# Hybrid attention block on one core: the state space's phasor step is squared once on GpSimd, and the first layer's parameters are issued later

## The chip, the cores and the metric

The kernel runs on one core of a Trainium2 chip. The metric is the device time of one execution in microseconds, from the program's start to its end. Three runs of the kernel before gave 1392.8, 1395.85 and 1401.91 us; the median is 1395.85 us.

## What is computed

Two layers of a hybrid block over 528 positions (16 meta tokens and 512 of the sequence) and 1024 channels. Each layer normalises, projects to three mixers (stick-breaking attention, retention, a state-space mixer), projects back, and adds a gated MLP. The part that the change touches is the state-space mixer:

```python
dt = jnp.exp(log_dt.astype(f32))[:, None]
mag = jnp.exp(lr * dt)
ar = mag * jnp.cos(li * dt)
ai = mag * jnp.sin(li * dt)
...
bu_r = jnp.einsum('lbgc,gpc->lbgp', ug, bbr)
bu_i = jnp.einsum('lbgc,gpc->lbgp', ug, bbi)
_, _, xr, xi = lax.associative_scan(_complex_affine_combine, (a_r, a_i, bu_r, bu_i), axis=0)
y = (jnp.einsum('lbgp,gcp->lbgc', xr, c_re.astype(f32))
     - jnp.einsum('lbgp,gcp->lbgc', xi, c_im.astype(f32)))
```

## The kernel before, in words

All activations are held transposed, channels on partitions and the 528 positions along the free dimension, in 60 shared slots. Matrix products of the weights are made in three passes (`mm3`: weight and input are each split into a rounded and a remaining part), in two halves of 264 columns; their accumulators are called `pj`. Weights come one unit at a time by DMA on SP's queue into two buffers (`wr`), are rounded on ScalarE (`wh`) and their rest taken on VectorE or GpSimd (`wl`).

A layer runs 23 units of projection in the order of `PROJ`, then the output projection in three parts (`OUT_PARTS`; in layer 0: stick-breaking, state space, retention), then the MLP. Everything else is written as generators (`spawn`), and `tick`, called after each weight product, resumes those that are due. Whether one is due goes by a clock that the building program keeps for each engine: `spend` adds the estimated duration of each instruction, and a task may go on once its own time is not later than TensorE's clock plus 200. So the estimates set the order in which instructions are written; after that the tile framework orders them once more, by a simulated time line with that order as priority, and each engine executes its list in order.

`first_params` (line 1046) runs from the start of the kernel: `s5_scalars` makes cosine, sine and magnitude of the states for both layers at once on VectorE (16 columns, 8 for each layer; `cu`, `su`, `mg`, in tiles `s5w` and `s5p`), then `s5_params` for layer 0 loads the matrices (`braw`) and starts five tasks: `inputs` twice (`btmp`, `ws`, `wps`, `we`), `outputs` (`gx`, `gg`, `bbd`, `kps`, `tz`) and `phasors` twice, one for each half of the states. For layer 0 the first half goes to VectorE and the second to GpSimd; layer 1's parameters are computed during layer 0's MLP, both halves on GpSimd.

`phasors` builds the powers of the chunk step's phasor, 132 of them for each state, by doubling: it holds the step's current power in `st` (4 columns), multiplies the powers so far (`phr`, `phi`, by way of `py`) by it, and squares it (lines 684 to 689). The list `par` is filled when all five tasks are over, and the state-space lane `s5_lane` of the layer (`uc`, `es`, `xr`, `xi`, `yps`, `ysm`, then `glu`) waits for it. The attention of a pair of heads waits for `sq`, `sk`, `sv` of that pair (the first two normed by `headnorm`); its scores are made in `z`, those of the retention in `sc` and its result in `ro`.

Of the kernel before, what the change touches and what calls it, by code (L numbers as in the profile page):

```python
# [8 lines left out]
F32 = mybir.dt.float32  # L9
# [3 lines left out]
ALU = mybir.AluOpType  # L13
PSUM = bass.MemoryType.PSUM

P = 128
# [21 lines left out]
NCH = T // Q  # L38
# [12 lines left out]
def width(g):  # L51
    return g[-1][3] + g[-1][2] - g[-1][1]
# [36 lines left out]
def hybrid_kernel(ctx, tc, A, out, dbg=None):  # L89
# [6 lines left out]
    def spend(key, ns):  # L96
        t = now[0]
        start = max(busy[key], busy["PE"])
        if t:
            if key != t[3]:  # L100
                t[3], t[4] = key, t[1]
            start = max(start, t[4])
            t[1] = max(t[1], start + ns + HOP)
        busy[key] = start + ns
# [21 lines left out]
    G = Timed(nc.gpsimd, "G", 110, 2.1)  # L126

    def mm(out, lhsT, rhs, start, stop, more=False):

        n = out.shape[-1] / 2.4  # L130
        spend("PE", 2 * max(107.0, 2 * n) if rhs.dtype == F32 else max(107.0, n) + 3)
        nc.tensor.matmul(out, lhsT=lhsT, rhs=rhs, start=start, stop=stop, skip_group_check=more)  # L132

    class TE:
# [5 lines left out]
    cp = ctx.enter_context(tc.tile_pool(name="cp", bufs=1))  # L140
# [12 lines left out]
    def nm(s):  # L153
        uid[0] += 1
        return f"{s}_{uid[0]}"

    def tt(s="t"):
        return tp.tile([P, T], F32, tag="t", name=nm(s))
# [58 lines left out]
    def const(shape, dt, name):  # L217
        return cp.tile(shape, dt, tag=name, name=name)
# [9 lines left out]
    for name, g in (("A", G_A), ("B2", G_B2)):  # L228
        n = width(g)
        m = masks[n] = const([P, n], BF16, "mask" + name)  # L230
        G.memset(m, 0.0)
        for j, q0, q1, o0 in g:
            c = slice(o0, o0 + min(q1 - q0, P))
# [111 lines left out]
    def mm3(ps, w, x, c0=0, nt=T, first=True, last=True, ticks=TICKS):  # L345

        a, b = w
        xh, xl = x
        kt = len(xh)
        for k in range(kt):  # L350
            for i, (wt, xt) in enumerate(((a, xh), (a, xl), (b, xh))):
                for p, (c, n) in zip(ps, spans(nt)):
                    mm(p[:, :n], lhsT=wt[:, k, :], rhs=xt[k][:, c0 + c:c0 + c + n],
                       start=first and k == 0 and i == 0, stop=last and k == kt - 1 and i == 2)
                tick(ticks)
# [24 lines left out]
    class Norm:  # L380
# [28 lines left out]
        def finish(self):  # L409
            a, b = self.acc  # L410
            for i in range(2):
                ps = bank("nps")
                c = slice(HALF * i, HALF * i + HALF)
                mm(ps[:, :HALF], lhsT=meanw, rhs=a[:, c], start=True, stop=False)
                mm(ps[:, :HALF], lhsT=meanw, rhs=b[:, c], start=False, stop=True)
                rs_from(ps[:, :HALF], self.rr, HALF * i, HALF)
            rs_exp(self.rr)
# [32 lines left out]
    def s5_scalars():  # L450
# [79 lines left out]
        mul(fi, t1, den)  # L530
        return cu, su, mg, ar, ai, fr, fi

    def s5_params(l, engines, scal, par):

        def on(eng):
            return (lambda o, a, b, op=op: eng.tensor_tensor(out=o, in0=a, in1=b, op=op)
                    for op in (ALU.mult, ALU.add, ALU.subtract))

        cu, su, mg, ar, ai, fr, fi = scal
        m_ = lambda t, a: t[:, 16 * a + 8 * l:16 * a + 8 * l + 8]  # L540
        fr, fi = m_(fr, 0), m_(fi, 0)
        braw = tt("braw")
# [26 lines left out]
        mul, add, sub = on(engines[0])  # L569
# [88 lines left out]
        def phasors(hf):  # L658

            eng = engines[hf]  # L660
            mul, add, sub = on(eng)
            p3 = lambda t: t.rearrange("p (t n) -> p t n", n=NCH)
            pr, pi, y1, y2 = tt("phr"), tt("phi"), tt("py"), tt("py")
            for t, v in ((pr, 1.0), (pi, 0.0)):
                G.memset(p3(t)[:, :, 0:1], v)
            st = cp.tile([P, 16], F32, tag=f"st{hf}", name=nm("st"))
            sr, si = st[:, 0:4], st[:, 4:8]
            ua, ub = st[:, 8:12], st[:, 12:16]
            eng.tensor_copy(out=sr, in_=m_(cu, 4)[:, 4 * hf:4 * hf + 4])
            eng.tensor_copy(out=si, in_=m_(su, 4)[:, 4 * hf:4 * hf + 4])  # L670
            n = 1
            while n < NCH:
                yield
                c = min(n, NCH - n)
                bs = lambda a: a.rearrange("p (t o) -> p t o", o=1).to_broadcast([P, 4, c])
                a1, a2 = p3(y1)[:, :, :c], p3(y2)[:, :, :c]
                mul(a1, p3(pr)[:, :, 0:c], bs(sr))
                mul(a2, p3(pi)[:, :, 0:c], bs(si))
                sub(p3(pr)[:, :, n:n + c], a1, a2)
                mul(a1, p3(pr)[:, :, 0:c], bs(si))  # L680
                mul(a2, p3(pi)[:, :, 0:c], bs(sr))
                add(p3(pi)[:, :, n:n + c], a1, a2)
                n *= 2
                if n < NCH:
                    mul(ua, sr, sr)
                    mul(ub, si, si)
                    mul(si, sr, si)
                    sub(sr, ua, ub)
                    add(si, si, si)
            ph[hf] = (pr, pi)  # L690
            over.append("phasors")

# [3 lines left out]
        for g in (inputs(0), inputs(1), outputs(), phasors(0), phasors(1)):  # L696
            spawn(g, now[0][1])
# [348 lines left out]
    def first_params():  # L1046
        yield
        scal.extend(s5_scalars())
        yield
        yield from s5_params(0, (V, G), scal, par)  # L1050

    scal = []
    spawn(first_params())
    for l in range(LAYERS):
        got = {}
# [95 lines left out]
        for n, (kind, i, f0, nf) in enumerate(mlp_order()):  # L1151
# [17 lines left out]
            if n == 3 and not last:  # L1169
                par = []  # L1170
                spawn(s5_params(l + 1, (G, G), scal, par), busy["G"])
# [101 lines left out]
```

## Time and profile before

| | |
|---|---|
| median of three runs | 1395.85 us (1392.8 to 1401.91) |
| the profiled execution's own time | 1399.35 us |
| its span, first to last instruction | 1397.6 us |
| mean granted TensorE clock | 0.990 |
| TensorE busy | 1370.0 us |
| VectorE busy | 807.1 us |
| ScalarE busy | 618.9 us |
| GpSimd busy | 509.2 us |

In the profile's rows PE is TensorE's matrix product and PEld its weight load, DVE is VectorE, ACT ScalarE, POOL GpSimd, SP the queue that issues the DMAs. Nearly all instructions of VectorE, ScalarE and GpSimd are recorded by one helper (line 121) and all matrix products by another (line 132), so they are told apart by the names of their tiles: `out<-in`.

### The profile page before, as it was taken

Reading aid. Unit: us, or ns where it says so; the run is one execution under the profiler, and the core shown is the slowest. Engines: PE = TensorE matmul, PEld = TensorE weight load, DVE = VectorE, ACT = ScalarE, POOL = GpSimd, SP = SyncE. Lnnn points to the kernel's source line nnn. Section 1 sums busy time; section 2 is a strip of 40 time slices with the busy share of each in tenths; the row PEclk is TensorE's granted clock in tenths of the full one; section 3 lists DMA queues with packets and bytes.
Section 4 is the critical chain, followed back from the end, with each engine's and each line's share of the span. In section 5 each row is a group of like instructions: output and inputs, shape, how many; then the busy total and the mean of one; then the engine's idle time right before and its main releaser. Section 6 shows DMA issues by size and latency. Waiting matters only on the chain.

```text
span 1397.6 us, 22767 instructions
## 1 busy us (share of the span) xinstructions
PE 1370.0 (98%) x9188; PEld 1254.3 (90%) x9188; DVE 807.1 (58%) x1312; ACT 618.9 (44%) x1002; POOL 509.2 (36%) x624
## 2 busy tenths in 40 slices
PE   6999999999999999999999999999999999999998
PEld 6989898999999999999999999998788888888886
DVE  8875557767455545544566477464585543553453
ACT  5456565545343223322354564874363432442231
POOL 5685536322689302200233544362122210220020
PEclk9999799999999999999999999999999999999999
DMA  4212102313221322222222121122232322223223
GB/s 154 69 65 96 38 21 84 97 46 115 97 76 61 106 91 91 90 93 87 80 91 91 61 93 46 56 68 82 79 106 96 100 92 94 101 91 104 93 77 105
DMA packets 38985, 118.27 MB, mean 85 GB/s; under 512 B 4960, under 2 KB 5472, under 8 KB 38880
## 3 DMA queue, kind: packets, MB, share of 16 engines
q1 hardware_dynamic: 38880, 116.82, 25.8%
q8 instruction: 72, 1.18, 0.3%
q14 instruction: 33, 0.27, 0.1%
HBM read 111.46 MB, written 2.10 MB: 81 GB/s over the span
## 4 chain that ended last, share of the span: by engine, by line
PE 85%; DVE 8%; POOL 4%; issue 1%; DMA 1%; ACT 1%; SPq 0%; DVEq 0%; POOLq 0%; ACTq 0%
PE pj L132 71%; PE z L132 6%; PE hps L132 1%; PE ro L132 1%; PE av L132 1%; DVE s5w L121 1%; PE sc L132 1%; PE yps L132 1%; DVE wl L121 1%; POOL lo L121 1%; PE kps L132 1%; DVE sq L121 1%; DVE gg L121 1%; DVE fr L121 0%; PE kv L132 0%
## 5 line engine op out<-in xcount | busy, mean ns | idle before, releaser
L132 PE MATMUL pj<-xh,wh 128*128 128x264 f32 (+1 forms) x1792 | 451.5, 311 | 13.7 <-ACT wh L121 5.2
L132 PE MATMUL pj<-xh,wl 128*128 128x264 f32 (+1 forms) x1792 | 451.6, 311 | 1.6 <-DVE wl L121 1.6
L132 PE MATMUL pj<-xl,wh 128*128 128x264 f32 (+1 forms) x1792 | 449.7, 310 | 1.7 <-DVE xl L121 1.7
L121 ACT CAST wh<-wr 128x1024 fp32r<-128x1024 f32 (+3 forms) x209 | 206.0, 987 | 417.5 <-PE pj L132 381.8
L132 PEld LDWEIGHTS pj<-xh,wh 128*128 128x128 f32 x1792 | 298.3, 191 | 31.3 <-issue 7.5
L132 PEld LDWEIGHTS pj<-xl,wh 128*128 128x128 f32 x1792 | 298.5, 190 | 19.6 <-DVE xl L121 2.4
L132 PEld LDWEIGHTS pj<-xh,wl 128*128 128x128 f32 x1792 | 298.2, 190 | 19.3 <-issue 2.0
L121 DVE TENSOR_TENSOR wl<-wr,wh 128x1024 fp32r<-128x1024 f32 (+3 forms) x166 | 249.2, 1502 | 73.7 <-ACT wh L121 71.3
L132 PE MATMUL pj<-hi,wh 128*128 128x264 f32 (+1 forms) x720 | 192.9, 323 | 0.0
L132 PE MATMUL pj<-lo,wh 128*128 128x264 f32 (+1 forms) x720 | 192.3, 321 | 0.0
L132 PE MATMUL pj<-hi,wl 128*128 128x264 f32 (+1 forms) x720 | 191.7, 321 | 0.1
L121 POOL TENSOR_TENSOR up<-ga,up 128x528 f32<-128x528 f32 (+1 forms) x44 | 61.8, 1405 | 345.6 <-DVE up L121 345.6
L121 DVE TENSOR_TENSOR h<-h,pj 128x264 f32<-128x264 f32 (+1 forms) x144 | 69.2, 511 | 135.1 <-PE pj L132 135.0
L121 POOL TENSOR_TENSOR wl<-wr,wh 128x1024 fp32r<-128x1024 f32 (+2 forms) x43 | 95.6, 2223 | 130.4 <-ACT wh L121 122.9
L132 PEld LDWEIGHTS pj<-hi,wh 128*128 128x128 f32 x720 | 119.4, 188 | 11.0 <-ACT wh L121 0.6
L132 PEld LDWEIGHTS pj<-hi,wl 128*128 128x128 f32 x720 | 119.4, 188 | 10.9 <-DVE wl L121 0.5
L132 PEld LDWEIGHTS pj<-lo,wh 128*128 128x128 f32 x720 | 119.4, 188 | 10.3
L121 POOL TENSOR_TENSOR lo<-ga,hi 128x528 fp32r<-128x528 f32 (+1 forms) x44 | 58.9, 1339 | 158.7 <-ACT hi L121 158.6
L121 DVE TENSOR_TENSOR up<-pj,R 128x264 f32<-128x264 f32 (+1 forms) x66 | 32.2, 515 | 95.2 <-PE pj L132 95.2
L121 ACT ACTIVATE si<-si,bias 128x528 f32<-128x528 f32 (+1 forms) x44 | 32.1, 731 | 94.3 <-DVE si L121 94.3
L121 DVE TENSOR_TENSOR ga<-si,up 128x528 f32<-128x528 f32 (+1 forms) x44 | 31.7, 720 | 72.7 <-ACT si L121 56.8
L121 ACT ACTIVATE e<-z 128x512 f32<-128x512 f32 (+2 forms) x72 | 39.3, 546 | 63.2 <-PE z L132 57.2
(228 smaller groups left out, 1747.1 us busy)
## 6 DMA issues: line engine op xcount, KB each, us to landing
wr<-in_w_in_dram SPq DMA_DIRECT2D x45, 512.0 KB, 3.5
wr<-in_w_gate_dram SPq DMA_DIRECT2D x44, 512.0 KB, 3.4
wr<-in_w_up_dram SPq DMA_DIRECT2D x44, 512.0 KB, 3.4
wr<-in_w_down_dram SPq DMA_DIRECT2D x32, 512.0 KB, 3.4
wr<-in_w_out_dram SPq DMA_DIRECT2D x16, 384.0 KB, 3.2
wr<-in_w_down_dram SPq DMA_DIRECT2D x16, 384.0 KB, 3.1
rc<-in_rope_dram SPq DMA_DIRECT2D x12, 264.0 KB, 3.7
rs<-in_rope_dram SPq DMA_DIRECT2D x12, 264.0 KB, 4.0
```

The source lines that it names most:

```text
L121: return f(*a, **k)
L132: nc.tensor.matmul(out, lhsT=lhsT, rhs=rhs, start=start, stop=stop, skip_group_check=more)
```

## The change

Three edits. The squarings of the step's phasor leave `phasors`; a new function `s5_steps` makes the eight powers at once for all 16 columns (both layers, both halves) on GpSimd, right after the scalars, and `phasors` reads them from its tile `s5s`. `first_params` then goes on to `s5_params` only when `sq` and `sk` of pair 0 are in `got`, that is, normed. And the building program's estimate for a matrix product with 64 rows or 64 output partitions is halved.

```diff
     def mm(out, lhsT, rhs, start, stop, more=False):
 
         n = out.shape[-1] / 2.4
-        spend("PE", 2 * max(107.0, 2 * n) if rhs.dtype == F32 else max(107.0, n) + 3)
+        t = 2 * max(107.0, 2 * n) if rhs.dtype == F32 else max(107.0, n) + 3
+        spend("PE", t / 2 if 64 in (rhs.shape[0], out.shape[0]) else t)
...
+    def s5_steps(scal):
+
+        W = 16
+        steps = cp.tile([P, 8 * 2 * W], F32, tag="s5s", name="s5s")
+        tmp = cp.tile([P, 2 * W], F32, tag="s5t", name="s5t")
+        ua, ub = tmp[:, :W], tmp[:, W:]
+        at = lambda i, c: steps[:, W * (2 * i + c):W * (2 * i + c) + W]
+        for c in range(2):
+            G.tensor_copy(out=at(0, c), in_=scal[c][:, 4 * W:5 * W])
+        for i in range(1, 8):
+            r, m = at(i - 1, 0), at(i - 1, 1)
+            G.tensor_tensor(out=ua, in0=r, in1=r, op=ALU.mult)
+            G.tensor_tensor(out=ub, in0=m, in1=m, op=ALU.mult)
+            G.tensor_tensor(out=at(i, 0), in0=ua, in1=ub, op=ALU.subtract)
+            G.tensor_tensor(out=ua, in0=r, in1=m, op=ALU.mult)
+            G.tensor_tensor(out=at(i, 1), in0=ua, in1=ua, op=ALU.add)
+        return steps
...
-            st = cp.tile([P, 16], F32, tag=f"st{hf}", name=nm("st"))
-            sr, si = st[:, 0:4], st[:, 4:8]
-            ua, ub = st[:, 8:12], st[:, 12:16]
-            eng.tensor_copy(out=sr, in_=m_(cu, 4)[:, 4 * hf:4 * hf + 4])
-            eng.tensor_copy(out=si, in_=m_(su, 4)[:, 4 * hf:4 * hf + 4])
             n = 1
-            while n < NCH:
+            for i in range(8):
                 yield
                 c = min(n, NCH - n)
+                o = 32 * i + 8 * l + 4 * hf
+                sr, si = steps[:, o:o + 4], steps[:, o + 16:o + 20]
...
                 n *= 2
-                if n < NCH:
-                    mul(ua, sr, sr)
-                    mul(ub, si, si)
-                    mul(si, sr, si)
-                    sub(sr, ua, ub)
-                    add(si, si, si)
...
         scal.extend(s5_scalars())
         yield
+        scal.append(s5_steps(scal))
+        yield lambda: ("sq", 0) in got and ("sk", 0) in got
         yield from s5_params(0, (V, G), scal, par)
```

## Rows read from the trace of the kernel before

**Rows 1.** The page: busy us by engine; the chain that ended last.

```profile
...
PE 1370.0 (98%) x9188; PEld 1254.3 (90%) x9188; DVE 807.1 (58%) x1312; ACT 618.9 (44%) x1002; POOL 509.2 (36%) x624
...
PE 85%; DVE 8%; POOL 4%; issue 1%; DMA 1%; ACT 1%; SPq 0%; DVEq 0%; POOLq 0%; ACTq 0%
...
```

**Rows 2.** Busy us by stretch: length, each engine (instructions), clock, DMA share, GB/s.

```profile
...
34.00:110.00 76.00, 71.37 (x538) 66.70 (x537) 58.59 (x155) 37.04 (x67) 58.80 (x125) 1.00 0.20 67
...
154.00:158.00 4.00, 2.86 (x20) 2.23 (x18) 4.00 (x5) 1.31 (x4) 4.00 (x3) 1.00 0.32 116
158.00:176.00 18.00, 18.00 (x77) 16.11 (x76) 4.07 (x13) 9.54 (x20) 7.44 (x7) 0.53 0.09 29
...
381.00:391.00 10.00, 6.42 (x33) 6.24 (x33) 6.90 (x10) 3.07 (x4) 9.77 (x16) 0.66 0.16 55
...
740.00:980.00 240.00, 239.37 (x1802) 224.51 (x1801) 145.05 (x261) 144.94 (x277) 107.62 (x76) 1.00 0.22 70
...
```

**Rows 3.** What TensorE waited for: us in total, times, longest us.

```profile
...
PE pj L132 <- DVE ga L121: 3.6, 1, 3.6
...
PE pj L132 <- DVE py L121: 2.0, 1, 2.0
...
PE vps L138 <- DVE rg L121: 1.1, 1, 1.1
...
PE kps L132 <- POOL bbd L121: 0.8, 1, 0.8
...
PE z L132 <- DVE u L121: 0.8, 1, 0.8
...
```

**Rows 4.** Tile st, 30:110 and 400:475 us: ns min/median/max, first, last start.

```profile
...
L121 POOL TENSOR_TENSOR st<-st x39: 188/200/249, 32.1 to 106.6; 128x4 f32<-128x4 f32 x39
L121 DVE TENSOR_TENSOR st<-st x35: 147/157/2351, 32.4 to 86.5; 128x4 f32<-128x4 f32 x35
...
L121 POOL TENSOR_TENSOR st<-st x66: 188/197/1326, 408.0 to 463.7; 128x4 f32<-128x4 f32 x66
...
```

**Rows 5.** VectorE in order of time: start, us, what, idle before.

```profile
...
33.90 2.33 DVE L121 TENSOR_TENSOR s5w<-s5p,cols 128x16 f32<-128x16 f32 x1
...
43.47 3.48 DVE L121 TENSOR_TENSOR gx<-braw,s5p 128x640 f32<-128x640 f32 x2 [3.62 <-DMA braw<-in_bc_dram]
...
53.30 0.76 DVE L121 SCALAR_TENSOR_TENSOR sq<-sq,cols,hsq 128x528 f32<-128x528 f32 x1
...
60.95 1.15 DVE L121 SCALAR_TENSOR_TENSOR sk<-sk,cols,hsq 128x528 f32<-128x528 f32 x1
...
```

**Rows 6.** GpSimd in order of time, 28 to 100 us.

```profile
...
33.80 2.40 POOL L121 TENSOR_TENSOR wl<-wr,wh 128x1024 fp32r<-128x1024 f32 x1 [1.09 <-ACT wh L121]
...
43.14 2.40 POOL L121 TENSOR_TENSOR wl<-wr,wh 128x1024 fp32r<-128x1024 f32 x1 [6.79 <-ACT wh L121]
...
72.01 0.21 POOL L121 TENSOR_TENSOR py<-phi,st 128x16 f32<-128x16 f32 x1
...
```

**Rows 7.** SP's DMA issues in order of time, 0 to 420 us.

```profile
...
38.22 0.42 SPq L543 DMA_DIRECT2D braw<-in_bc_dram  x1
45.57 79.22 SPq L283 DMA_DIRECT2D wr<-in_w_in_dram  x9
...
```

**Rows 8.** ScalarE in order of time, 38 to 62 us.

```profile
...
50.72 0.67 ACT L121 ACTIVATE hsq<-hsq 128x528 f32<-128x528 f32 x1
...
```

**Rows 9.** TensorE, then VectorE, in order of time near 150 us.

```profile
...
140.93 2.03 PE L132 MATMUL z<-sq,sk 64*128 64x256 f32 x10
...
150.63 2.39 DVE L121 TENSOR_TENSOR xi<-fr,phi 128x528 f32<-128x528 f32 x1
152.94 1.62 DVE L121 TENSOR_TENSOR y<-fi,phr 128x528 f32<-128x528 f32 x1
...
```

**Rows 10.** Tile glu until 310 us; VectorE in order of time after 300.

```profile
...
L121 DVE TENSOR_TENSOR lo<-glu,hi x2: 698/698/699, 287.4 to 288.1; 128x528 fp32r<-128x528 f32 x2
...
304.19 0.77 DVE L121 TENSOR_TENSOR h<-h,pj 128x264 f32<-128x264 f32 x2 [4.27 <-PE pj L132]
...
```

## What the change was expected to do

> **What bounds the kernel now.** I read the page first, then the busy time by stretch, then TensorE's waits, and only then single instructions of the stretches that stood out. TensorE is busy for 98% of the span and carries 85% of the chain that ended last [rows 1]. The change adds no matmul and takes none away, so it can only give back, or add, time in which TensorE idles or runs at its lower clock. That time is small and lies in few places [rows 2]. From 34 to 110 us, where the first layer's parameters are computed, 76.00 - 71.37 = 4.6 us are idle. From 154 to 158 us 1.14 us are idle, and right behind it TensorE runs 18 us at a mean granted clock of 0.53, which is the 1.2 GHz level for most of it: 18 x 0.47 = 8.5 us lost. Around 381 us, in the first layer's MLP, 3.6 us are idle and the clock is 0.66 for the 10 us: 3.4 us more. The second layer's projections and attention, the same code in another order, lose 0.6 us in 240. So some 18 us could come back after the start-up, and 1% is 14 us.
>
> The waits name the causes [rows 3]: 2.0 us on `py` and 0.8 us on `u` (VectorE, in the stretch of the phasors), 1.1 us on `rg` (the idle time ahead of the slow clock), 3.6 us on `ga` (the MLP), 0.8 us on `bbd` (GpSimd, second layer's parameters).
>
> **Part 1, the squarings.** In the kernel before each of four phasor tasks squares its step 7 times (NCH is 132), in 5 instructions each: 35 on VectorE and 35 on GpSimd for layer 0, 70 on GpSimd for layer 1. The counts agree: 35 on VectorE, 39 + 66 = 105 on GpSimd [rows 4]. At the medians the removal is 35 x 0.157 = 5.5 us of VectorE and 105 x 0.20 = 21 us of GpSimd, of which 14 us fall into the MLP. Eight copies go too (6 on GpSimd, 2 on VectorE, under 0.3 us each). Added are 35 products and 2 copies of 128x16 on GpSimd, before anything else of the parameters. The nearest row is a 128x16 product on GpSimd, 0.21 us [rows 6]: 37 x 0.21 = 7.8 us in one dependent chain. It can start where the old squarings did, at 32.1 us [rows 4], and GpSimd has nothing but one `wl` of 2.40 us until 43.1 (6.79 us idle before that one) [rows 6]. 32.1 + 7.8 + 2.4 = 42.3: it fits in the gap, cost nothing. Without that cover the cost is at most 7.8 us of start for the parameters, which have the slack worked out in part 2.
>
> VectorE pays for GpSimd's work, though. A 128x16 product of the scalars took 2.33 us beside GpSimd's 2.40 us `wl` [rows 5, 6]. If each of the 37 new GpSimd products held VectorE for its own length, the last scalars and the reads of the first projections out of PSUM, which follow them on VectorE, would come up to 7.8 us later; the scalars are nearly done by then, so I keep half of it, +4, for the range and take 0, because TensorE's waits on VectorE in that stretch are for `py` and `u` alone, far behind [rows 3]. The Trainium skill ("GPSIMD Engine Reference", Key points) says that GpSimd shares its SBUF interfaces with VectorE and contends with VectorE instructions that have two SBUF inputs; the 2.33 us agree with that. By that rule alone moving small products to GpSimd is no relief for VectorE, and the forecast would be 4 us higher.
>
> What do the 5.5 us bring in layer 0? They are taken from between the PSUM reads that TensorE waited for: bound 0 (another VectorE instruction ends last) to 2.0 + 0.8 = 2.8 us. In layer 1 the 14 us of GpSimd are in the MLP, where TensorE waits once, 0.8 us for `bbd`: bound 0 to 0.8; I take all of it, because `bbd`'s copies stand among the squarings on the same queue.
>
> **Part 2, the wait.** Now `braw` is asked for at 38.2 and the first product `gx` starts at 43.5 [rows 5, 7]. With the wait the load and everything behind it (products for the input and output matrices, transposes, `kps`, phasors) is issued after `sq` and `sk` of pair 0 are normed. The norm of `sk` is at 60.95, but the exponential that it needs was done at 50.72 + 0.67 = 51.4 [rows 5, 8]: 9.5 us were lost behind parameter products, and `sq` had the like at 53.3. Freed of these, `sk` is done near 52. The load stands in SP's queue behind weight loads that each wait for a free buffer; the next nine took 79 us to issue, 8.8 us each [rows 7], so it moves by one or two places: 45.6 to 54 us. The parameters then start 8 to 16 us later (I take 10), and the last phasor step, near 106.6 now [rows 4], ends at 106 + 10 - 7 (35 x 0.20 that GpSimd no longer does) = 109, at worst 116. Queued behind the load on SP are weights, with three units of lead.
>
> Who waits for the parameters? The state-space lane of layer 0, which ends with `lo` of `glu` at 288.8; TensorE takes up those rows only for the second part of the output projection. The last sum of the first part into `h` is at 304.2 [rows 10]. Slack 15 us: +3 (or +10) costs nothing.
>
> What does TensorE gain early? VectorE keeps all the parameter work but 5.5 us; it only runs it later, between the PSUM reads of pairs 1 and 2. Both ends: 0 to 2.8 us as above. I take 1.0, since most of the work that delays the reads is only moved.
>
> What is late next is the jam at 150 us. The wait for `rg` comes from two state-space products on VectorE, `xi` 2.39 us and `y` 1.62 us beside GpSimd work [rows 9], that stand ahead of the read of `rg`. Their lane now comes some 3 to 10 us later against the projections, and the order around it changes too (part 3). I take the idle 1.1 us and the slow stretch of 8.5 us as gone: -9.6; the other end is 0.
>
> **Part 3, the price of a 64-row matmul.** No instruction changes, but the program that writes the kernel advances its TensorE clock by half as much for the products of `z`, `sc` and `ro`. Per layer that is 6 x 2.64 (three `G_A`, two `G_B1`, three `G_B2` matmuls a head) + 3 x 2.14 + 3 x 2.14 = 28.7 us before, 14.3 now. Ten such matmuls of `z` took 2.03 us [rows 9]; the old price of the ten is 3.47 us, the new one 1.74. So the new price is nearer, and every due time in both attentions moves: the order of instructions there is redrawn, that of the MLP is not. What an order is worth is bounded by the two layers: 9.6 us lost to one jam in layer 0, 0.6 in layer 1 [rows 2]. So 0 to -9.6 for layer 0 (the same jam as in part 2, not a second gain) and 0 to +9.6 for layer 1. I take 0 here.
>
> **Sum.** Against the profiled execution's own 1399.35 us (span 1397.6 and 1.75 around it; 3.5 above the median 1395.85): -1.0 -0.8 -9.6 = 1388.0 us.
>
> **Rivals.**
> A, the forecast: the slow stretch at 158 us goes, the MLP's stop stays. 1388, own range 1383 to 1393.
> B, the slow stretch stays, or an equal one appears elsewhere in layer 0: the work only moves. For it: VectorE and GpSimd keep nearly all their work in this layer. Against it: the products that made it are moved. 1399.35 - 1.8 = 1397.5. That the change does nothing at all (the load would come late anyway) gives the same.
> C, the MLP's stop at 381 us goes as well: 1388 - 3.6 - 3.4 = 1381. For it: GpSimd is full there. Against: the squarings come after 404 us (first at 408.0 [rows 4]), the stop before them.
> D, slower: the state-space lane is the late one. It decides from the point where it ends more than 15 us later than now; with parameters 25 us late TensorE idles 10 us before the second part of the output projection and, as at 381 us, runs slowly behind it, 3.4: 1397.5 + 13.4 = 1411. Against it: I find 3 to 10 us.
> E, slower: the new order gives layer 1 a jam like that of layer 0 while layer 0 keeps its own: 1397.5 + 9.6 = 1407.
>
> **Chances.** A 0.40, B 0.27, C 0.14, D 0.07, E 0.12. The median before may hold fewer slow stretches than the profiled execution (it is 3.5 us below), which spreads A and B by as much. 1380 to 1406 leaves out the lower part of C (0.07), most of D (0.06) and the upper part of E (0.06). A measurement of this kernel can tell about 1%, 14 us, from no change: faster means below 1381.9 (half of C and the lower edge of A, 0.13), slower above 1409.8 (half of D and the edge of E, 0.07), same 0.80.
>
> **What would show it.** Right: 37 products of 128x16 on GpSimd before the first `gx`, no `st` rows of the phasors; `gx` first at 51 to 60 us; the norms of `sq` and `sk` before 53; last phasor step at 106 to 116; no stretch at 0.5 clock between 150 and 180; the idle time near 381 us unchanged; the same PE instructions, 9188. Wrong: parameters later than 120 us, a clock below 0.9 in any stretch of layer 1, idle TensorE near 300 us, or new idle time between 60 and 110 us above 5 us.

## The result, and the profile after

The changed kernel takes 1407.24 us (median of 12, 1403.0 to 1410.79) against 1395.7 us before in the same session (median of 12): ratio 1.0085, 95% interval 1.0067 to 1.0104. It is slower by 11.5 us; the forecast was 1388.0 us, and 1407.24 lies just outside the range of 1380 to 1406. The profiled execution's own time is 1410.79 us, its span 1409.1 us, mean granted clock 0.984.

Of the 12 executions the profiled one took longest; its span, too, is 11.5 us longer than the one before (1397.6). Where these went is read from the first `nps` matmul of each stage, the sums of a norm (us, one profiled execution each):

| | start | layer 0, mixers | layer 0, MLP | layer 1, mixers | layer 1, MLP |
|---|---|---|---|---|---|
| before | 34.6 | 311.3 | 394.2 | 298.5 | 359.0 |
| after | 36.2 | 316.0 | 398.4 | 297.7 | 360.8 |

The kernel after, busy us by stretch (columns as in [rows 2]):

```profile
...
34.00:110.00 76.00, 71.09 (x464) 66.93 (x464) 53.56 (x108) 37.11 (x68) 53.27 (x102) 0.87 0.18 60
...
88.00:108.00 20.00, 19.23 (x78) 18.04 (x79) 5.81 (x18) 7.59 (x14) 7.67 (x17) 0.50 0.08 26
...
158.00:176.00 18.00, 18.00 (x151) 17.88 (x150) 14.35 (x25) 9.48 (x17) 12.71 (x12) 1.00 0.25 83
300.00:314.00 14.00, 12.15 (x62) 9.69 (x61) 4.74 (x11) 6.84 (x14) 1.31 (x1) 0.63 0.00 0
386.00:396.00 10.00, 6.40 (x40) 6.21 (x39) 6.91 (x10) 2.61 (x4) 9.85 (x15) 0.83 0.19 54
428.00:440.00 12.00, 8.40 (x45) 7.01 (x44) 3.38 (x5) 3.60 (x5) 11.76 (x27) 0.72 0.29 89
750.00:990.00 240.00, 239.37 (x1799) 224.33 (x1799) 141.90 (x262) 145.15 (x276) 105.05 (x75) 1.00 0.22 69
...
```

The 1.6 us of the first column cannot be put down to the change: over the 20 kernels of the next table that column lies between 34.0 and 37.7 us. The slow stretch of 158 to 176 us [rows 2] is gone: clock 1.00. One of the same size stands at 88 to 108 us, at 0.50 (the 1.2 GHz level), 19.23 x 0.50 = 9.6 us lost. New are the slow stretch at 300 to 314 us and the stop at 430 us. Layer 1's mixers are as clean as before. TensorE's waits after (to be held against [rows 3]):

```profile
...
PE pj L133 <- DVE ga L121: 3.6, 1, 3.6
PE kps L133 <- POOL bbd L121: 3.6, 1, 3.6
...
PE pj L133 <- DVE sq L121: 3.1, 1, 3.1
...
PE pj L133 <- DVE rg L121: 1.2, 1, 1.2
PE hps L133 <- ACT hsq L121: 1.1, 1, 1.1
...
```

`py` is gone, `sq` has come (VectorE reads a projection out of PSUM at 88.29 us, TensorE goes on at 88.77), and `bbd` went from 0.8 to 3.6 us. The three stops that matter here, TensorE in order of time, after:

```profile
...
88.77 0.59 PE L133 MATMUL pj<-xh,wh 128*128 128x264 f32 x1 [3.13 <-DVE sq L121]
...
301.37 1.32 PE L133 MATMUL ro<-sc,rv 128*64 128x128 f32 x10 [0.73 <-DVE sc L121]
...
307.76 2.12 PE L133 MATMUL hps<-hsq,blk 128*128 128x264 f32 x4 [1.09 <-ACT hsq L121]
...
```

VectorE and GpSimd around the wait for `sq`, in order of time, after:

```profile
...
78.46 0.23 DVE L121 TENSOR_TENSOR py<-phr,s5s 128x64 f32<-128x64 f32 x1
78.60 2.43 DVE L121 TENSOR_TENSOR py<-phi,s5s 128x64 f32<-128x64 f32 x1
80.95 0.76 DVE L121 TENSOR_TENSOR u<-pj,R 128x264 f32<-128x264 f32 x2
...
83.46 1.32 DVE L121 TENSOR_TENSOR py<-phi,s5s 128x64 f32<-128x64 f32 x1
...
88.29 0.42 DVE L121 TENSOR_TENSOR sq<-pj,R 128x264 f32<-128x264 f32 x1
...
```

```profile
...
78.53 2.42 POOL L121 TENSOR_TENSOR wl<-wr,wh 128x1024 fp32r<-128x1024 f32 x1 [0.24 <-ACT wh L121]
...
81.30 5.49 POOL L121 TENSOR_TENSOR lo<-sp,hi 128x432 fp32r<-128x432 f32 x5
...
```

Pair 0's attention, now ahead of the parameters, puts five `lo` on GpSimd at 81.3 us; beside them phasor products of 128x64 on VectorE take 0.9 to 1.3 us, where the one at 78.46 us takes 0.23, and the read of `sq` stands behind them.

### The profile page after: what moved, and what is told of

Same layout as the page of the kernel before. It is cut to its first block, busy times and chain, and to the rows that moved or that the text cites. A ratio compares the mean times of both kernels' runs of the same rounds, so it can differ in the third digit from the quotient of the medians.

```text
span 1409.1 us, 22670 instructions
## 1 busy us (share of the span) xinstructions
PE 1375.4 (98%) x9188; PEld 1258.3 (89%) x9188; DVE 800.1 (57%) x1275; ACT 620.3 (44%) x1002; POOL 491.1 (35%) x550
## 3 DMA queue, kind: packets, MB, share of 16 engines
q8 instruction: 72, 1.18, 0.3%
## 4 chain that ended last, share of the span: by engine, by line
PE 88%; DVE 6%; POOL 3%; issue 1%; ACT 1%; DMA 0%; SPq 0%; DVEq 0%; POOLq 0%; ACTq 0%
PE pj L133 73%; PE z L133 7%; PE hps L133 2%; PE ro L133 2%; PE av L133 1%; POOL py L121 1%; DVE s5w L121 1%; PE yps L133 1%; PE sc L133 1%; DVE py L121 1%; PE kps L133 1%; DVE wl L121 0%; PE es L133 0%; POOL lo L121 0%; POOL gx L121 0%
## 5 line engine op out<-in xcount | busy, mean ns | idle before, releaser
L133 PE MATMUL pj<-xl,wh 128*128 128x264 f32 (+1 forms) x1792 | 454.6, 311 | 2.7 <-DVE xl L121 2.7
L121 ACT CAST wh<-wr 128x1024 fp32r<-128x1024 f32 (+3 forms) x209 | 206.1, 988 | 433.8 <-PE pj L133 392.2
L121 DVE TENSOR_TENSOR wl<-wr,wh 128x1024 fp32r<-128x1024 f32 (+3 forms) x166 | 244.2, 1472 | 74.1 <-ACT wh L121 70.2
L121 POOL TENSOR_TENSOR up<-ga,up 128x528 f32<-128x528 f32 (+1 forms) x44 | 62.0, 1409 | 359.8 <-DVE up L121 355.6
L121 ACT ACTIVATE e<-z 128x416 f32<-128x416 f32 (+2 forms) x72 | 39.1, 546 | 52.1 <-PE z L133 51.2
```

The costliest lines, as they stand in the source:

```text
L121: return f(*a, **k)
```

## The experiments

All kernels in one table. "wps" is the first `we` (ScalarE's copy of the parameters' transposes), "ssm" and "ret" the last `lo` of `glu` and of `o` (ends of the state-space and the retention lane), "MLP at" the first `nps` of the first MLP, "MLP" its length, "bbd" TensorE's wait for it; all us, one profiled execution each. The ratio is to the kernel before on the same chip, with its interval; in it 0.001 is 1.4 us. The places come from one execution: that of the changed kernel, of e6_layer0_only, of e11 and of e6_price_wait was the longest of its kernel (by 3.6, 5.2, 5.0 and 3.2 us over the median), so there they may lie some us late.

| kernel | ratio | wps | ssm | ret | MLP at | MLP | bbd |
|---|---|---|---|---|---|---|---|
| before | 1 | 70.6 | 288.1 | 311.2 | 345.9 | 394.2 | 0.8 |
| after | 1.0085 (1.0067-1.0104) | 100.3 | 307.0 | 318.1 | 352.2 | 398.4 | 3.6 |
| e1_price | 0.9994 (0.9978-1.0009) | 70.0 | 289.4 | 313.1 | 340.0 | 393.1 | 1.3 |
| e2_squarings | 1.0068 (1.0048-1.0087) | 107.8 | 302.9 | 312.7 | 346.8 | 397.9 | 3.6 |
| e3_wait | 1.0002 (0.9985-1.002) | 100.2 | 300.2 | 311.7 | 343.4 | 392.8 | 1.4 |
| e4_sq_wait | 1.0077 (1.0057-1.0097) | 98.1 | 294.9 | 321.6 | 348.2 | 398.3 | 3.5 |
| e5_chain_unused | 1.0033 (1.0018-1.0047) | 108.5 | 297.2 | 320.8 | 347.4 | 393.3 | 1.2 |
| e6_layer0_only | 1.0041 (1.0025-1.0056) | 107.1 | 311.6 | 321.5 | 355.6 | 393.7 | 1.2 |
| e7_layer1_only | 1.0061 (1.0044-1.0077) | 109.9 | 297.4 | 321.0 | 347.6 | 396.9 | 3.6 |
| e8_bbd_early | 1.003 (1.0017-1.0042) | 100.2 | 304.1 | 315.4 | 349.5 | 392.0 | - |
| e9_chain_unpriced | 0.9994 (0.9978-1.001) | 71.3 | 284.6 | 307.8 | 342.4 | 394.7 | 1.1 |
| e10_clock_only | 1.0051 (1.0031-1.0071) | 111.4 | 304.6 | 312.1 | 347.5 | 393.3 | 1.4 |
| e11_sq_unpriced | 1.0061 (1.0038-1.0083) | 72.9 | 304.6 | 319.9 | 349.7 | 397.5 | 3.6 |
| e12_price_sq_unpriced_early | 1.0001 (0.9984-1.0019) | 72.2 | 282.1 | 305.9 | 340.8 | 392.8 | - |
| e6_price_wait | 1.0155 (1.013-1.0179) | 100.9 | 316.5 | 340.5 | 367.8 | 392.9 | 1.2 |
| e13_price_sq_early | 0.9993 (0.9981-1.0006) | 97.3 | 294.3 | 310.8 | 340.7 | 392.2 | - |
| e14_price_gv | 0.9995 (0.998-1.001) | 70.7 | 292.4 | 316.1 | 343.1 | 392.6 | - |
| e15_price_sq_gv | 1.0054 (1.0035-1.0072) | 70.0 | 286.8 | 310.7 | 345.3 | 396.7 | - |
| e16_e13_ggup | 0.9971 (0.9956-0.9985) | 99.3 | 296.4 | 312.9 | 342.8 | 389.5 | - |
| e17_e12_ggup | 1.0001 (0.9985-1.0017) | 70.5 | 283.5 | 307.3 | 342.0 | 390.7 | - |

The times that missed what was expected: e2, e7 and e10 came 0.4 to 1.5 us above theirs (1406.5, 1405.4, 1404.3 us), e6_layer0_only (1404.3) and e16 (1392.0) between the two ranges given, e15 (1403.1) 7 us above both, e6_price_wait (1417.3) 14 us above; e11 and e17 are taken up below.

### One part alone: e1_price, e2_squarings, e3_wait, e4_sq_wait

Each is the kernel before with the hunks of the change named: the two lines of `mm`; `s5_steps` and the new loop of `phasors`; the line with `got`; the last two together.

> Only the halved estimate for 64-row products; squarings in place, no wait. Theory P (the estimate redraws the order, and the new order makes the new stops): TensorE idles near 81 to 89 us and runs at 0.5 clock behind it, and the time is near that of the changed kernel, 1404 to 1409 us. Theory W (the wait brings pair 0's attention forward into the phasors and so makes the stop at 85 us): no idle time above 2 us between 80 and 110 us, first z near 80 us as before, time 1393 to 1398. Theory S (the squarings at once shift GpSimd's work in the MLP): no stop at 430 us here, kps waits at most 1 us; time 1393 to 1398.

> Only the squarings, made once on GpSimd; no wait, old estimate. Theory S: the stop of 3.6 us on bbd near 430 us and the half clock behind it are there, 3.6 + 3.3 = 7 us, and the parameters of layer 0 start as late as in the changed kernel (bb products near 55 to 60 us); time 1400 to 1405. Theory P and theory W: no stop on bbd above 1 us; the jam at 150 to 176 us is as before; time 1393 to 1398.

> Only the wait for the norms of pair 0; squarings in place, old estimate. Theory W: the norms of sq and sk come by 52 us, the first z near 58 us instead of 80, the stop of some 3 us and 20 us at 0.5 clock between 81 and 110 us are there, those at 150 to 176 us are gone, time within 3 us of the kernel before (1393 to 1399). Theory P and theory S: first z near 80 us, jam at 150 us as before, time 1393 to 1398; the places tell them apart, not the time.

> Squarings and wait, old estimate: the change without its third edit. Theory P: the early stop at 81 to 110 us and the one at 430 us are gone or halved, time 1393 to 1399. Theory W with S: both stops are there, time 1403 to 1409, the estimate is worth nothing.

The estimate alone and the wait alone change nothing that can be measured; the squarings alone cost 0.68%, with the wait 0.77%, which is not told apart from 0.68. Theory P falls: an early stop (5.9 us, on `u`) is in e4 too, without the halved estimate. The wait does what theory W said, and where: in e3 the norms have started by 52 us, the first `z` is at 58.5, TensorE waits 6.4 us for `u` at 81 to 88 us, and the jam at 150 us is gone, with a net of nothing. The jam is no mark of the wait alone, though: e1 and e2 do not have it either (clock 1.00 from 158 to 176 us). Theory S holds as to `bbd`: 3.6 us in e2 and e4, 1.3 and 1.4 in e1 and e3. Its other half does not: in e2 GpSimd's chain does not keep VectorE's first `gx` back (42.7 us, before 43.5), and the `bb` products start at 48.9 us, not at 55 to 60.

### Which layer, and the chain itself: e5_chain_unused, e6_layer0_only, e7_layer1_only

```diff
-            n = 1
-            for i in range(8):
...
+            if False:
+                n = 1
+                for i in range(8):
...
+            else:
...
+                n = 1
+                while n < NCH:
...
```

The cut is from e5, against the changed kernel; e6_layer0_only has `if l == 0:` there and e7 `if l == 1:`. The first loop reads the steps from `s5s`, the second squares in `st` as before; all three go without the wait and with the old estimate.

> The kernel before, with the chain of 37 products and copies of 128x16 on GpSimd written out after the scalars, but not used: every phasor task squares for itself as before; no wait, old estimate. Theory C (the chain itself, in GpSimd's queue and beside VectorE, delays the first layer's parameters): the start and the first layer's mixers cost as much as with the squarings replaced, 3 to 6 us, the MLP's stop on bbd stays at 1 us or less: 1400 to 1403. Theory R (what costs is that the squarings are missing where they were, so that other work moves up): 1394 to 1399. The time of the 37 products that I forecast, nothing, says the same as R.

> The chain, used by the first layer's phasors; the second layer's square as before; no wait, old estimate. If the stop on bbd in the first layer's MLP comes from the second layer's missing squarings (theory R), the wait of kps on bbd is back at 1.5 us or less and the MLP takes 393 to 394.5 us instead of 398: 4 us less than with the squarings replaced in both layers, 1401 to 1403. If the stop comes from where the MLP begins or from the first layer's state (rival), it stays at 3.6 us and the time is 1405 to 1408.

> The chain, used by the second layer's phasors only; the first layer's square as before; no wait, old estimate. Theory R: the stop on bbd of 3.6 us is there with 2 to 3 us of half clock behind it, the first layer's mixers go as in the kernel with the chain unused; time 4 to 5 us over that kernel, 1400 to 1405. Rival: bbd waits 1.5 us at most, time as with the chain unused.

The parts add up: the chain, written but not used, +0.33%; used by layer 0, +0.08% more (within the intervals); used by layer 1, +0.28% more; by both, 0.68%. By e5 alone theory C would stand: the chain costs; whether by its time or by the order that it brings is the next pair's to say. The second layer's share is the stop on `bbd`: from e5 to e7 the MLP is 3.6 us longer (393.3, 396.9), the other stages stay within 0.7 us, and the medians differ by 3.7 us. The first matmul of `kps` in e7, then in e6 (TensorE in order of time):

```profile
429.87 0.63 PE L132 MATMUL kps<-gg,bbd 128*32 128x128 f32 x2 [3.60 <-POOL bbd L121]
```

```profile
437.70 0.41 PE L132 MATMUL kps<-gg,bbd 128*32 128x128 f32 x2 [1.17 <-POOL bbd L121]
```

### The stop on bbd: e8_bbd_early

```diff
+            if l:
+                copies()
...
-            bbd = [tt("bbd"), tt("bbd")]
...
+            if l == 0:
+                copies()
...
```

`copies` clears the two `bbd` and makes their four copies; the first call stands ahead of the `gx` products.

> The changed kernel, all three edits, with the second layer's bbd cleared and copied ahead of its gx products instead of behind the phasors that moved up. If the stop on bbd costs what the profile shows, 3.6 us idle and 2 to 3 us at half clock, the MLP falls from 398 to 392 to 394 us and the time from 1407 to 1400 to 1403. If something else on GpSimd or VectorE ends last there (rival), a stop of the same length appears on another tile of the parameters (gg, tz, ga) and the time stays 1405 to 1408.

As expected: no wait on `bbd` left, the MLP 392.0 instead of 398.4 us, the time down from 1.0085 to 1.0030. GpSimd after, in order of time, shows why the copies were late:

```profile
...
430.23 0.56 POOL L121 MEMSET bbd<- 128x256 f32 x2
430.73 0.54 POOL L121 MEMSET tz<- 128x528 f32 x1
431.23 1.27 POOL L121 TENSOR_TENSOR py<-phr,s5s 128x64 f32<-128x64 f32 x1
432.47 0.48 POOL L121 TENSOR_TENSOR py<-phi,s5s 128x64 f32<-128x64 f32 x1
432.91 0.32 POOL L121 TENSOR_TENSOR phi<-py,py 128x64 f32<-128x64 f32 x1
433.18 1.31 POOL L121 COPY bbd<-bb 64x128 f32<-64x128 f32 x4
...
```

The squarings left, and larger phasor products (128x64) took their place ahead of the copies. `kps` could go on 81.7 us after the MLP's first `nps` (433.86 - 352.2), as before (427.65 - 345.9 = 81.8). But TensorE came to it after 78.1 us instead of 80.9: `kps` stands 16 matmuls earlier in TensorE's list, as it does in e2, e4, e7 and e11, whose second layer does not square either. That the smaller estimate on GpSimd moved it there is the likely reason; it was not tried by itself. e8 moves `kps` ahead by another 54 matmuls, and it also takes away the 0.8 to 1.4 us that kernels without the stop wait for `bbd`; the early copies were not tried on the kernel before.

### The chain's time, or its entry in the clock: e9_chain_unpriced, e10_clock_only, e11_sq_unpriced

```diff
...
-            G.tensor_tensor(out=ua, in0=r, in1=r, op=ALU.mult)
+            nc.gpsimd.tensor_tensor(out=ua, in0=r, in1=r, op=ALU.mult)
...
+        for _ in range(37):
+            spend("G", 110 + 2.1 * 16)
...
```

The first lines are from `s5_steps` of e9 and e11: a call on `nc.gpsimd` itself makes no entry in the clock. The last two are e10: they stand in the kernel before, after the scalars.

> The kernel before with the unused chain of 37 products and copies on GpSimd, but issued without an entry in the building program's clock. The lists of instructions of the other engines are then those of the kernel before, in the same order; GpSimd has the chain more. Theory O (the chain costs only through the order: its 5.3 us in the building program's clock put the parameters' transposes wps behind the first attention scores z): wps near 70 us, ahead of z at 78, and 1395 to 1399, the same as before. Theory C (GpSimd's time and its contention with VectorE): 1400 to 1403, as with the priced chain.

> The kernel before with no instruction more or less: only the 37 entries of 144 ns for GpSimd are made in the building program's clock after the scalars. Theory O: wps falls behind the first z, we near 105 to 110 us instead of 71, the state-space lane starts 20 to 30 us later, waits of hps for hsq above 2 us between 230 and 270 us, and the time is 1400 to 1403. Theory C: 1394 to 1399.

> The squarings once for all states, used by both layers' phasors, without the wait, old estimate for 64-row products, and the chain without an entry in the building program's clock. Theory O: wps near 70 us, the first layer's mixers as before (306 to 312 us), and only the MLP's stop on bbd is left, 3.6 us idle and 2 to 3 at half clock: 1400 to 1403, some 5 us under the squarings with the priced chain. Theory C: 1405 to 1408.

e9 and e10 decide. In e9 GpSimd does the chain's work, and the lists of TensorE, VectorE, ScalarE and SP are the same as before, instruction by instruction: 0.9994. In e10 not one instruction is added; 37 x 0.1436 = 5.3 us in the building program's clock move the order, and the time rises by 0.51%. The rows by tile (instances, ns min/median/max, first and last start) of e9, then e10:

```profile
...
L121 ACT COPY we<-wps x4: 568/586/587, 71.3 to 77.0; 128x512 f32<-128x512 f32 x4
...
L132 PE MATMUL es<-uc,we x32: 273/276/359, 129.0 to 217.2; 128*128 128x132 f32 x32
...
L121 DVE TENSOR_TENSOR lo<-glu,hi x2: 694/694/695, 284.0 to 284.6; 128x528 fp32r<-128x528 f32 x2
...
```

```profile
...
L121 ACT COPY we<-wps x4: 569/583/593, 111.4 to 117.8; 128x512 f32<-128x512 f32 x4
...
L132 PE MATMUL es<-uc,we x32: 273/276/278, 161.0 to 251.9; 128*128 128x132 f32 x32
...
L121 DVE TENSOR_TENSOR lo<-glu,hi x2: 709/709/709, 303.4 to 304.6; 128x528 fp32r<-128x528 f32 x2
...
```

5.3 us of estimate put the parameters' transposes behind the first scores of the attention; they come 40 us later, the lane starts 32 us later and ends 20 us later. The expected waits for `hsq` were smaller (1.4 us); 5.0 us on `u`, 2.5 on `kt` and 1.7 on `lo` stand there instead. e11 was expected at 1400 to 1403 and gave 1404.4: `bbd` waits 3.6 us as expected, but with the squarings out of the first layer's phasors the lanes end late (304.6, 319.9) although `wps` is early. Not having the wait and not moving the transposes is not enough. And once the squarings are out, taking the entry away gains nothing that can be measured (e2 1.0068, e11 1.0061): its price of 0.33 to 0.51% is shown only where the phasors still square for themselves.

### The rest of the loss: e12_price_sq_unpriced_early, e6_price_wait, e13_price_sq_early

e12 is e11 with the halved estimate and `bbd` early; e6_price_wait the kernel before with the halved estimate and the wait; e13 the changed kernel without the wait and with `bbd` early.

> Squarings once for both layers, chain without an entry in the clock, halved estimate, no wait, and the second layer's bbd copied ahead of its gx products. If the two causes (parameters behind the scores; bbd behind the phasors) are all that the change lost, nothing is left of the loss: no stop on bbd, wps near 70 us, 1390 to 1397. If something else of the change costs, it stays above 1400.

> Halved estimate and wait, squarings in place. If the wait under the new estimate costs the rest of the changed kernel's loss in the first layer, 1399 to 1403 with idle time on u or sq near 81 to 89 us and half clock behind it; if wait and estimate are both harmless without the new chain, 1393 to 1399, with no waits of hps for hsq above 1 us near 300 us.

> The changed kernel without the wait, and with the second layer's bbd copied early; the chain keeps its entry in the clock. If the wait holds the 4 us that remain once bbd is cured, 1394 to 1398; if the chain's place does, 1400 to 1404, with wps behind the first z and waits of hps for hsq between 230 and 310 us.

With the wait out and `bbd` early nothing of the loss is left, whether the chain is in the clock (e13) or not (e12). So in the changed kernel the other 0.30% hang on the wait: e8 and e13 differ by nothing else. Under the new estimate and without the wait the chain's entry costs nothing (e13 against e12); with the wait it was not tried. In the traces two stretches go with the wait. One is the stop on `sq`: from 80 to 110 us e8 idles 4.1 us, e13 not at all; but e13 idles 4.3 us from 230 to 270 us, where e8 idles 1.2. The other is not made good: from 298 to 309 us TensorE has only products of the retention, with the stops on `sc` and `hsq` shown above, and from 300 to 314 us the changed kernel is busy for 12.15 us at a clock of 0.63, e8 for 12.91 at 0.61, e13 for 14.00 at 1.00. And wait and halved estimate, each harmless alone, cost 1.55% together, more than either theory gave; the squarings, put to these two, take 0.7% of that back (1.0085). The wait costs only under the halved estimate: under the old one it adds nothing that can be measured (e3 to the kernel before, e4 to e2). TensorE of e6_price_wait in order of time:

```profile
...
293.73 1.01 PE L133 MATMUL ro<-sc,rv 128*64 128x128 f32 x4 [4.48 <-DVE sc L121]
...
315.77 0.81 PE L133 MATMUL pj<-hi,wh 128*128 128x264 f32 x2 [6.95 <-ACT hi L121]
...
```

The second line is the output projection's second part waiting for `hi` of `glu`; the next matmul in TensorE's list needs it.

### The MLP's other stop: e14_price_gv, e15_price_sq_gv, e16_e13_ggup, e17_e12_ggup

```diff
...
-                spawn(s5_params(l + 1, (G, G), scal, par), busy["G"])
+                spawn(s5_params(l + 1, (G, V), scal, par), busy["G"])
...
+                if ri and l:
+                    SC.activation(x1, x1, AF.Copy, scale=-1.0)
...
-                        if ri:
+                        if ri and l == 0:
...
-            G.tensor_tensor(out=b[:, :nt], in0=a[:, :nt], in1=b[:, :nt], op=ALU.mult)
+            (V if not last and 2 <= i < 5 else G).tensor_tensor(out=b[:, :nt], in0=a[:, :nt], in1=b[:, :nt], op=ALU.mult)
...
```

The first two lines are e14 (on e1) and e15 (on e12, with `bbd` in its old place), the rest e16 (on e13) and e17 (on e12); the branch that `l == 0` leaves out for layer 1 is `sub(o, a, b)` on GpSimd.

> The kernel before with the halved estimate, and the second half of the second layer's parameters on VectorE instead of GpSimd, so that the four gg products on VectorE no longer wait for gx on GpSimd. If the stop on ga near 380 us is that wait, its 3.7 us and the 2 to 3 us at half clock behind it go: the MLP falls from 393 to 387 to 389 us, 1388 to 1392 in all. If VectorE, with the new work, holds up the reads of the MLP instead, new waits on ga or up appear between 375 and 450 us and the time is 1395 to 1402.

> Halved estimate, squarings once for both layers with the chain unpriced, no wait, and the second half of the second layer's parameters on VectorE. bbd is left in its place. If the share on VectorE cures both stops of the MLP, ga and bbd, 1386 to 1391; if bbd stays behind the phasors, 3.6 us on bbd and 1392 to 1396.

> The kernel of e13 (halved estimate, squarings once, chain in the clock, no wait, bbd early); in addition the second layer's four gg products of the second kind are made on GpSimd (ScalarE turns the sign), and three of the MLP's products up<-ga,up on VectorE. If the stop on ga is VectorE waiting for GpSimd ahead of the reads, its 3.8 us and the 3 us at half clock behind it go: MLP 392 to 386, 1387 to 1390. If it is VectorE's own load, the wait stays on another tile and the time 1393 to 1398.

> The kernel of e12 (halved estimate, squarings once, chain not in the clock, no wait, bbd early) with the same two moves. Same expectations: stop gone and 1387 to 1390, or 1393 to 1398; the two should differ from each other by less than 2 us, as e12 and e13 do.

Half the parameters on VectorE does not help: `ga` waits 4.3 us in e14, now behind VectorE's own `gx`, `gg` and `btmp`; in e15 the stops on `bbd` and `ga` are gone, but `wps` waits 7.5 us for `ws`, and the time is 0.54% above before. Taking away VectorE's two waits for GpSimd does remove `ga`, but not all of the gain stays. TensorE's waits in e16 (36 to 460 us):

```profile
...
PE hps L133 <- ACT hsq L121: 4.6, 3, 2.5
PE wps L139 <- POOL ws L121: 2.4, 1, 2.4
...
```

No `ga`, but 2.4 us on `ws`, behind the `gg` that GpSimd now makes. e16 gives 1391.98 us, 0.9971 (0.9956 to 0.9985): faster than before by 0.3%, than the changed kernel by 1.1% (by their ratios). e17, with the same two moves, gives 1.0001: the profile shows the MLP 2.1 us shorter than in e12 (390.7, 392.8) and the time the same. That e16 and e17 differ by 3.5 us was not expected and is not explained; what goes with it is the clock, 0.994 to 0.998 in the twelve executions of e16, 0.988 to 0.997 in those of e17.

## Why the prediction was wrong

Three steps of the prediction failed where the changed kernel pays. Its term of -0.8 us for `bbd` has the wrong sign: the stop grew to 3.6 us, and 0.55 of the 0.85% go with it (e8). Its sentence that a later lane "costs nothing" left out that the wait and the halved estimate redraw one order together: the wait costs the other 0.30% (e8 against e13). And its largest term, -9.6 us for the jam, came to nothing. The steps one by one:

- **Part 1, layer 0, "cost nothing".** GpSimd had the room: e9 shows the chain's time to be worth nothing (0.9994, 0.9978 to 1.001). The step that failed counted the chain only as time on GpSimd and not as an entry in the building program's clock, though I knew that this clock sets the order: by itself +0.33% (e5), or +0.51% without any instruction (e10). The size was off too. The chain ran from 31.9 to 50.9 us, not to 42.3 (after, by tile):

```profile
...
L121 POOL TENSOR_TENSOR s5t<-s5s x21: 210/220/1170, 32.2 to 50.3; 128x16 f32<-128x16 f32 x21
L121 POOL TENSOR_TENSOR s5s<-s5t x14: 213/220/683, 36.5 to 50.7; 128x16 f32<-128x16 f32 x14
...
```

  In the changed kernel the entry is not what costs, as far as the runs show: with the squarings out it is worth nothing under the old estimate (e11 against e2) or, without the wait, under the new one (e12 against e13). The chain did not stand before the first `gx` (44.4 us) either, which was a sign named for "right".

- **Part 1, the bound of +4 from contention** was rightly not taken: e9 has the chain beside the same VectorE list, and the ratio is 0.9994. The Trainium skill ("GPSIMD Engine Reference", Key points) has GpSimd contend with VectorE instructions of two SBUF inputs; the rows at 78 to 88 us agree with it, in single instructions, but in the chain's place it reaches no wait of TensorE.

- **Part 1, layer 1, "-0.8 for bbd".** Wrong sign: 3.6 us idle, and the clock at 0.72 for the 12 us around it (8.40 x 0.28 = 2.4 us). The step "`bbd`'s copies stand among the squarings on the same queue" took it that what is removed ahead of an instruction brings it forward. Phasor products moved up instead, and `kps` moved ahead in TensorE's list. It is worth 3.6 us of the MLP between e5 and e7, 6.4 us between the changed kernel and e8, which also loses the wait that the kernel before has.

- **Part 2, the wait.** Right: the norms (`sq` 47.2, `sk` 51.2 us). Wrong: `braw` is asked for at 38.9 us (before 38.2); that the wait carries no data, so that the framework's second ordering is free to undo it for a load, is the likely reason and was not tested; `gx` starts at 44.4, not at 51 to 60, and the last phasor step at 122.8 instead of 106 to 116. What moved is the rest: `z` ahead, the transposes behind it. I took the lane to be 10 us late by its load; it was late by its transposes. The rows by tile of before, then after:

```profile
...
L121 ACT COPY we<-wps x4: 568/587/587, 70.6 to 77.0; 128x512 f32<-128x512 f32 x4
...
L132 PE MATMUL z<-sq,sk x96: 176/376/793, 78.7 to 225.4; 64*128 64x256 f32 x36, 64*128 64x144 f32 x24, 64*128 64x16 f32 x24, 64*128 64x272 f32 x12
...
L132 PE MATMUL es<-uc,we x32: 274/276/359, 129.2 to 220.5; 128*128 128x132 f32 x32
...
```

```profile
...
L121 ACT COPY we<-wps x4: 586/587/589, 100.3 to 114.0; 128x512 f32<-128x512 f32 x4
...
L133 PE MATMUL z<-sq,sk x96: 176/330/793, 57.9 to 217.7; 64*128 64x256 f32 x36, 64*128 64x144 f32 x24, 64*128 64x16 f32 x24, 64*128 64x272 f32 x12
...
L133 PE MATMUL es<-uc,we x32: 273/276/359, 166.5 to 246.0; 128*128 128x132 f32 x32
...
L121 DVE TENSOR_TENSOR lo<-glu,hi x2: 689/699/709, 302.6 to 307.0; 128x528 fp32r<-128x528 f32 x2
...
```

  The lane starts 37 us later (`es`) and ends 19 us later (307.0 against 288.1 [rows 10]): past the 15 us that rival D named as its point. So "slack 15 us: +3 (or +10) costs nothing" failed by its size; what TensorE then lost near 300 us is told under e13.

- **"-9.6, the jam is gone".** It is gone from 150 us, and e3 shows that the wait does that (so does the halved estimate alone, e1). From 34 to 110 us 4.9 us are idle (before 4.6) and 71.09 x 0.13 = 9.2 us are lost to the clock (before none). That is rival B's "an equal one appears elsewhere": the term is zero, and so is the -1.0 for early waits (`py` and `u` go from 2.8 to 0.9 us, `sq` brings 3.1). The term was also too large from the start, since it was read from one execution. e9, whose TensorE list is that of the kernel before, has the same stop (1.18 us on `rg`) and loses 18 x 0.28 = 5.0 us behind it, not 8.5. Of 115 executions of the kernel before, 12 have a mean clock of 0.997 or 0.998 (the profiled one 0.990), so they cannot have lost 8.5 us there; they take 1391.4 us in the mean, 5 to 6 us below the medians of 1396.3 to 1397.8. And e1, e3 and e13, at clock 1.00 from 158 to 176 us, come to ratios of 0.9994, 1.0002 and 0.9993: in none of them did the missing jam make the kernel measurably shorter. The forecast took its 11.4 us from an execution that stood 3.7 us above the median of its session.

- **Part 3, the halved estimate, took 0.** Alone 0.9994, so right; but its bound (0 to -9.6 us for layer 0) is wrong for it together with the wait (1.0155, 21 us longer). The edits do not add: I worked out each against the order before. "The new price is nearer" is a misreading as well: the trace has 96 rows of `z` in layer 0 (above) where the program writes 6 heads x 8 = 48 matmuls, so each stands as two rows. The ten rows of 2.03 us are five matmuls, old price 1.74 us, new 0.87: the old price was the nearer one, and the third edit took the clock away from what is measured.

- **A sum.** The stretches named at the start give 4.6 + 1.1 + 8.5 + 3.6 + 3.4 = 21.2 us, not "some 18"; the 3.4 counts idle time again (6.42 x 0.34 = 2.2). The forecast does not use either.

- **Right as well:** 9188 matmuls, the MLP's stop on `ga` unchanged at 3.6 us, layer 1 never below a clock of 0.9. Of the signs named for "wrong", two came: parameters later than 120 us (122.8) and idle time near 300 us (14.00 - 12.15 = 1.9 us).

- **The rivals.** D's lane came true and I gave it 0.07; its 10 us of idle time did not (1.9 us, on `sc` and `hsq`, not on `glu`). The table tells how far it goes, by two limits that were drawn after it was made: where "ssm" is by 300.2 and "ret" by 316.1, the MLP starts at 340.0 to 343.4 us, save before and e15 (345.9, 345.3), which run for most of 18 us at half clock near 160 us (0.53, 0.62); in the ten others one of the two lanes is later, and it starts at 346.8 to 367.8. Late transposes alone do not do it: e3, e13 and e16 have them at 97 to 100 us and lose nothing. E's size fits (1407), its place does not: layer 1 runs at clock 1.00. No rival had the MLP's new stop, though 0.55 of the 0.85% go with it (e8).

- **Open.** Which instruction makes a lane late differs from kernel to kernel (`u`, `kt`, `sc`, `hsq`); no single wait was found that they share. That the late lane makes the later MLP is shown directly only in e6_price_wait (6.95 us), elsewhere it is read from the table.

## What to carry to other kernels

Where a program orders its instructions by estimates, an added instruction has two prices, its time and its entry in that clock; price the second by writing the entry without the instruction and the instruction without the entry. Work removed ahead of a late instruction need not bring it forward: ask what will move up into the gap, and whether its consumer moves ahead too. Several edits that each redraw an order are one edit: forecast and test them together.

## What the runs showed of the hardware

How long TensorE stays at the 1.2 GHz level behind a stop does not follow the length of the stop. Idle 1.1 us before 158 us was followed by 18 us at 0.53 [rows 2], and by 0.72 over the same 18 us in e9, where TensorE has the same instructions in the same order and idled 1.2 us; 3.1 us before 88.8 us by 20 us at 0.50 in the kernel after; the 12 us around the stop of 3.6 us at 430 us have a mean of 0.72. A dependent chain of 128x16 products on GpSimd advances by 0.30 us a link, though one product is shown with 0.22 us (after, GpSimd in order of time):

```profile
...
36.18 0.22 POOL L121 TENSOR_TENSOR s5t<-s5s 128x16 f32<-128x16 f32 x1
36.48 0.22 POOL L121 TENSOR_TENSOR s5s<-s5t 128x16 f32<-128x16 f32 x1
36.78 0.22 POOL L121 TENSOR_TENSOR s5t<-s5s 128x16 f32<-128x16 f32 x1
...
45.25 2.96 POOL L121 TENSOR_TENSOR wl<-wr,wh 128x1024 fp32r<-128x1024 f32 x1
...
```

The prediction had taken 0.21 us for each, and one `wl` of 2.40 us where two came.
